# The product of probabilities and values with the probabilities stationary, in an encoder with linear and attention heads on one core

## The chip, the core and the metric

The kernel runs on one core of one Trainium2 chip. The metric is device time in microseconds of one execution, lower is better; the median of a few runs is taken. TensorE (PE) multiplies: it loads a stationary operand (PEld in the profile) and streams a moving one past it into PSUM. VectorE (DVE), ScalarE (ACT) and GpSimd (POOL) do the rest of the arithmetic, SyncE (SP) issues the DMAs.

## The reference

Two layers, each on 2048 tokens of 1024 channels. A normalised row is projected to several groups of columns; one half of the result is a gated mix inside chunks of 128 tokens, the other half is attention with 8 query heads of 64 channels on 2 key/value heads. Both halves are gated, projected back, normalised and added to the input. The part that is changed lies in the attention:

```python
def attend(qblk):
    sc = jnp.einsum('bqkgd,bskd->bkgqs', qblk, k).astype(jnp.float32) * scale
    p = jax.nn.softmax(sc, axis=-1).astype(v.dtype)
    return jnp.einsum('bkgqs,bskd->bqkgd', p, v)
...
y_b = gqa_axial_attention(q, k, v, q_norm_g[l], k_norm_g[l], tables) * jax.nn.silu(g_b)
y = jnp.concatenate([y_a, y_b], axis=-1)
out = jnp.einsum('bse,ed->bsd', y, w_out[l])
x = x + rmsnorm(out, post_g[l])
```

All of it is float32. The kernel reaches that precision by splitting operands in a high and a low half and adding the products of the halves.

## The kernel before

For each layer the kernel first projects (class `Project`) and keeps keys, values and queries; the values are scaled by a power of two and split in f16 halves (`scale_v`): `v16` holds, per key tile and key/value head, 64 high and 64 low columns. Then comes the attention (`attend`).

The attention runs over 32 units: 4 query blocks of 512 queries times 8 heads. A unit has 16 key tiles of 128 keys, so one layer has 512 steps (`k` in the loop). In each step TensorE makes scores with the keys on the partitions (`sp`, 128 keys by 512 queries, two matmuls), ACT takes the exponential twice, once to f16 (`p_hi`) and once to float32 (`p_f`), and POOL, in 15 of 100 steps DVE, forms the low half `p_lo` = `p_f` - `p_hi` (`sub_lo`). Three steps later (`LAG`, `LAG_LO`) the product with the values follows.

In that product the values are stationary and the probabilities stream, 512 columns at a time: per key tile one matmul with all 128 columns of `v16` and `p_hi`. It leaves in `s.po` a 128 by 512 result, the high values' part on one half of the partitions and the low values' part on the other. Every eight key tiles (`BATCH`) the products with `p_lo` follow, for the eight tiles at once, in products of 32 stationary columns: two of them per tile with the high values, into the right half of `s.po`, and two with a block of ones (`one_h`), into the bank `sums`, one for `p_lo` and one for `p_hi`. Four such products take four different strips of 32 columns of the array and run beside each other. So the denominators lie along the free axis of `sums`.

At the end of a unit `finish` evacuates: `half` (ACT) copies one half of `s.po`, `whole` (DVE) adds the other, `den_t` (DVE) transposes `sums` in blocks of 32, `den` (TensorE) sums and scales the denominators by small products with `two` into a bank `pd` with the queries on the partitions, `rden` (DVE) takes the reciprocal, `gate` (DVE) multiplies the gate by it, and for each pair of heads `gate_t` (TensorE) transposes the gate, `mul` (DVE) multiplies, and `split` (ACT and POOL) makes the halves `y_hi` and `y_lo`, which are stored.

Between these, spread over the steps, stand: the maxima of later units (`max_step`: one matmul `pmax` of 512 columns and one reduction on DVE, 16 per unit, in four of five steps), the output projection of the block before (`out_steps`, matmuls `pout`, taken from the list `fill`), and its normalisation (`post_steps`, one DVE instruction per step from `post_queue`).

The order of the work is written out by hand: `Pinned` keeps each instruction of TensorE, ACT, DVE and POOL in program order. In one step `k` it is: the scores and exponentials of `k`; POOL's `sub_lo`; one of `post_queue`; DVE's `sub_lo` of `k - 1`; what was put in `later` for this step, `max_step` first, then what `finish` put there; some of `fill`; then the product of step `k - 3`. `finish(u, k + 1)` is called at the last product of unit `u`.

PSUM has eight banks of 512 float32 columns: seven in the pool `ps` (scores, maxima, `po`, `pout` and others take one when they are allocated), and `sums`.

Of the kernel before, what the change touches and what calls it, by code (L numbers as in the profile page):

```python
# [26 lines left out]
NKV = 2  # L27
EPS = 1e-6
WB = 256
C_U, C_VA, C_GA, C_Q, C_K, C_GB = 0, 512, 1024, 1536, 2048, 2304  # L30
RSQRT_MAGIC = float(0x5F3759DF)
EXP_SHIFT = 4.1588830833596715
# [6 lines left out]
def encoder(ctx: ExitStack, tc, x, w_in, w_out, pre_g, post_g, ln_a_g, ln_a_b,  # L39
# [50 lines left out]
    make_identity(nc, ident)  # L90
    ones1 = const.tile([1, P], F32, name="ones1")
    nc.vector.memset(ones1, 1.0)
    two = const.tile([P, 32], F32, name="two")
    nc.vector.tensor_tensor(two, ident[:, 0:32], ident[:, 32:64], ALU.add)
    nc.vector.tensor_tensor(two, two, ident[:, 64:96], ALU.add)
    nc.vector.tensor_tensor(two, two, ident[:, 96:P], ALU.add)
    nc.vector.tensor_scalar_mul(two, two, 2.0)
    one_h = const.tile([P, 32], F16, name="one_h")
    nc.vector.memset(one_h, 1.0)

    ws_d = dram.tile([P, 2, NH * P], F32, name="ws_d")
    xn_d = [[dram.tile([P, D], F32, name=f"xn_{l}_{t}") for t in range(NT)] for l in range(DEPTH - 1)]
# [64 lines left out]
            while self.jobs:  # L167
                self.jobs.pop(0)[1]()

    sums = psum.tile([P, GRP], F32, name="sums")  # L170

    bg = Background()
    PASSES = ((0, 0), (0, 1), (1, 0))
# [1 line left out]
    class Project:  # L175
# [23 lines left out]

        def gains(self):  # L200
            l = self.l
            self.two = lay.tile([P, 32], F32, name="two_v")
            self.gain_q = lay.tile([P, 2, HD], F32, name="gain_q")
            self.gain_k = lay.tile([P, 2, HD], F32, name="gain_k")
            for gain, src in ((self.gain_k, k_norm_g), (self.gain_q, q_norm_g)):
                nc.sync.dma_start(gain[:, 0, :], src[l].partition_broadcast(P))
                gv = gain[:, 1, :].rearrange("p (a h i) -> p a h i", a=2, h=2)
                sv = src[l].rearrange("(a h i) -> a h i", a=2, h=2)
                for h in range(2):
                    nc.sync.dma_start(gv[:, :, h, :], sv[:, 1 - h, :].partition_broadcast(P))  # L210
            top = small.tile([P, 2], F32, name="g_top")
            e = small.tile([P, 1], F32, name="g_exp")
            inv = small.tile([P, 1], F32, name="g_inv")
            nc.vector.tensor_reduce(top[:, 0:1], self.gain_k[:, 0], AX.X, ALU.max)
            nc.vector.tensor_reduce(top[:, 1:2], self.gain_k[:, 0], AX.X, ALU.min, negate=True)
            nc.vector.tensor_tensor(e, top[:, 0:1], top[:, 1:2], ALU.max)
            ei = e.bitcast(I32)
            nc.vector.tensor_scalar(ei, ei, EXP_BITS, None, ALU.bitwise_and)
            nc.vector.tensor_scalar(ei, ei, float(97 << 23), float(157 << 23), ALU.max, ALU.min)
            nc.vector.tensor_scalar(inv.bitcast(I32), ei, -1.0, float(254 << 23), ALU.mult, ALU.add)  # L220
            nc.vector.tensor_scalar(self.gain_k, self.gain_k, inv, None, ALU.mult)
            nc.vector.tensor_scalar(self.gain_q, self.gain_q, e, HD ** -0.5, ALU.mult, ALU.mult)
# [266 lines left out]
        def scale_v(self):  # L489
# [18 lines left out]
            def scale():  # L508
                nc.vector.tensor_copy(e, self.top[:, 0:1])
                ei = e.bitcast(I32)  # L510
                nc.vector.tensor_scalar(ei, ei, EXP_BITS, None, ALU.bitwise_and)
                nc.vector.tensor_scalar(ei, ei, float(64 << 23), None, ALU.max)
                nc.vector.tensor_scalar(ei, ei, -1.0, V_TOP, ALU.mult, ALU.add)
                nc.vector.tensor_scalar(self.two, two, e, None, ALU.mult)

            def apply(i):
                def f():
                    t = slice(4 * i, 4 * i + 4)
                    hi = v16[:, t, :, 0:HD]
                    nc.scalar.activation(hi, v32[:, t], AF.Copy, scale=e)  # L520
                    nc.vector.scalar_tensor_tensor(v16[:, t, :, HD:2 * HD], v32[:, t], e, hi, ALU.mult, ALU.subtract)
                return f

            bg.add(6, spread)
            bg.add(11, spread_row)
            bg.add(13, scale)
            for i in range(NT // 4):
                bg.add(14 + i, apply(i))

        def run(self, kv, first, last_jobs, first_wo):  # L530

# [108 lines left out]
    T_DELAY = 9  # L640
    VA_DELAY = 9
    LAG = 3
    LAG_LO = 3
    BATCH = 8
    N_HI = 12
    N_F = 4
    N_LO = 12
    LAST_0 = 5
    LAST_1 = 12
    WS_DELAY = 18  # L650
# [1 line left out]
    def attend(l, kv, nxt):  # L652
# [74 lines left out]
        def finish(u, k):  # L727
# [1 line left out]
            qb, h = units[u]  # L729
            side = h % 2  # L730
            s, pr = state[u], pairs[u // 2]
            r, o = slice(side * HD, (side + 1) * HD), slice((1 - side) * HD, (2 - side) * HD)

            def half():
                if side == 0:
                    pr.o = f_t("o_pair")
                ACT.copy(pr.o[r], s.po[o])

            def whole():
                DVE.tensor_tensor(pr.o[r], s.po[r], pr.o[r], ALU.add)  # L740

            def den_t():
                s.ds = f_t("den")
                DVE.transpose(s.ds, sums)

            def den():
                s.pd = ps_t("pd")
                rows = s.ds.rearrange("p (t c j) -> p t c j", c=4, j=32)
                for c in range(4):
                    PE.matmul(s.pd[32 * c:32 * c + 32, 0:TPG], layers[l].two, rows[:, :, c, 0], start=True, stop=True)  # L750

            def rden():
                s.rd = small.tile([P, TPG], F32, name="rden")
                DVE.reciprocal(s.rd, s.pd[:, 0:TPG])

            def gate():
                gv = pr.gb[:, :, r]
                DVE.tensor_tensor(gv, gv, s.rd.unsqueeze(2).broadcast_to([P, TPG, HD]), ALU.mult)

            def gate_t():  # L760
                pr.pg = ps_t("pg")
                for j in range(TPG):
                    PE.transpose(pr.pg[:, j * P:(j + 1) * P], pr.gb[:, j, :], ident)

            def mul():
                DVE.tensor_tensor(pr.o, pr.pg, pr.o, ALU.mult)

            def split():
                y_hi = f_t("y_hi", dt=F32R)
                y_lo = f_t("y_lo", dt=F32R)  # L770
                ACT.copy(y_hi, pr.o)
                (DVE if u + 1 == len(units) else POOL).tensor_tensor(y_lo, pr.o, y_hi.bitcast(F32), ALU.subtract)
                if (qb, h) == units[-1]:
                    last_y.extend([y_hi, y_lo])
                    return
# [2 lines left out]
                nc.sync.dma_start(y_d[qb][:, c, 1], y_lo.bitcast(F32))  # L778

            if u + 1 == len(units):  # L780
                for n, f in ((0, den_t), (0, den), (1, rden), (1, gate), (1, half), (1, whole), (2, gate_t), (2, mul),
                             (2, split)):
                    at(k + n, f)
                return
            at(k, half)
            at(k, whole)
            at(k, den_t)
            narrow.append(den)
            at(k + BATCH, rden)
            at(k + BATCH + 1, gate)  # L790
            if side == 0:
                return
            at(k + BATCH + 3, gate_t)
            at(k + BATCH + 4, mul)
            at(k + BATCH + 5, split)

        narrow = []
        post_queue = []
        last_y = []

# [245 lines left out]
                f()  # L1046

        yield before, first_wo
        both = [w_t([P, 8, GRP], "p_parts", F16) for _ in range(3)]
        both = [b[:, n] for b in both for n in range(8)]  # L1050
        his, los = both[:N_HI], both[N_HI:]
        fs = w_t([P, N_F, GRP], "p_f", F32)
# [38 lines left out]
        def weight(k):  # L1091
            return 2 if k >= total - 2 * NT else 1

        end = total + LAG_LO

        def sub_lo(k, engine):
            engine.tensor_tensor(p_lo(k), p_f(k), p_hi(k), ALU.subtract)
# [18 lines left out]
        for k in range(end + 4):  # L1116
# [27 lines left out]
            if 0 <= kb < total:  # L1144
                u, i = kb // NT, kb % NT
                s = state[u]
                kv = units[u][1] // (NH // NKV)
                if i == 0:
                    s.po = ps_t("po")
                PE.matmul(s.po, v16[:, i, kv, :], p_hi(kb), start=(i == 0), stop=False)  # L1150
            kb = k - LAG_LO
            if 0 <= kb < total:
                u, i = kb // NT, kb % NT
                s = state[u]
                kv = units[u][1] // (NH // NKV)
                if i % BATCH == BATCH - 1:
                    while narrow:
                        narrow.pop(0)()
                    for n in range(i - BATCH + 1, i + 1):
                        kn = kb - i + n  # L1160
                        q = n % 2 * HD
                        for c in range(0, HD, 32):
                            PE.matmul(s.po[q + c:q + c + 32], v16[:, n, kv, c:c + 32], p_lo(kn),
                                      start=False, stop=(n >= NT - 2))
                        q = HD - q
                        PE.matmul(sums[q:q + 32], one_h, p_lo(kn), start=(n < 2), stop=(n >= NT - 2))
                        PE.matmul(sums[q + 32:q + HD], one_h, p_hi(kn), start=(n < 2), stop=(n >= NT - 2))
                if i == NT - 1:
                    finish(u, k + 1)
                    if units[u][1] == NH - 1 and u + 1 < len(units):  # L1170
# [33 lines left out]
    for l in range(DEPTH):  # L1204
# [1 line left out]
        kv = [k_t[:, 0], k_t[:, 1]]  # L1206
        v_t = big_t([P, 2, NT * NKV * HD], "v_st")
        kv.append(v_t.bitcast(F32)[:, 0].rearrange("p (t k d) -> p t k d", t=NT, k=NKV))
        kv.append(v_t.bitcast(F16)[:, 1].rearrange("p (t k d) -> p t k d", t=NT, k=NKV))
        att = attend(l, kv, layers[l + 1] if l + 1 < DEPTH else None)  # L1210
        layers[l].run(kv, layers[l].first, *next(att))
        for _ in att:
# [41 lines left out]
```

## Time and profile before

| | |
|---|---|
| median of 3 runs | 2740.2 us (2739.36 to 2740.77) |
| span of the profiled execution | 2737.6 us |
| TensorE busy | 2666.4 us (97%), 18234 matmuls |
| weight loads busy | 1773.2 us (65%) |
| DVE busy | 1858.2 us (68%) |
| ACT busy | 1523.9 us (56%) |
| POOL busy | 1296.1 us (47%) |

The span is the profiled execution's own time, from its first instruction to its last; the runs' median, which has also what lies around the span, is 2.6 us more. The first stretch of attention lies between about 627 and 1373 us of the span, the second between 1977 and 2716; the projections lie before each. The page's busy time of TensorE is a union of its matmuls' durations, which overlap (a matmul of 512 columns is shown with 0.38 us, while the next starts 0.22 after it); so its cost is read from the starts, or from the chain of work, which gives each step the time up to the next. In the profile L84 is the helper that records the pinned instructions, so groups are told apart by their tiles: `po<-p_parts,v_st` is the product with the values, `sums<-p_parts,one_h` that with the ones, `sp` the scores, `p_parts` the f16 halves `p_hi` and `p_lo`.

### The profile page before, as it was taken

What the parts mean: (1) busy time and instruction counts of PE and PEld (TensorE: products, weight loads), DVE (VectorE), ACT (ScalarE), POOL (GpSimd) and SP (SyncE); (2) the same over time, 40 slices, a digit from 0 to 9 for tenths busy, and PEclk for the clock granted to TensorE, in tenths of its full rate; (3) what the DMA queues carried; (4) which work ended last, traced back from release to release, by engine and by line L of the source; (5) the groups of instructions that cost most, each with busy time, mean ns of one, the idle gap of its engine ahead of it and who ended that gap; (6) DMA issues with size and microseconds to landing.
All of it is one profiled execution on the core that took longest, in us unless ns stands there. A gap on an engine that the chain in (4) does not pass through costs nothing.

```text
span 2737.6 us, 48445 instructions
## 1 busy us (share of the span) xinstructions
PE 2666.4 (97%) x18234; PEld 1773.2 (65%) x18234; DVE 1858.2 (68%) x3780; ACT 1523.9 (56%) x3023; POOL 1296.1 (47%) x1079
## 2 busy tenths in 40 slices
PE   7999999999999999999999999999999999999997
PEld 7998999764444444445599989997644444444444
DVE  7762888876666766666497538897766656666664
ACT  5221422118887777877642224221388878778774
POOL 1210121008786776777633011210377767767764
PEclk9999999999999999999999999999999999999998
DMA  4434422322232222222354434232312222221313
GB/s 137 149 98 122 161 80 84 107 75 84 81 91 66 76 84 84 90 81 84 125 169 138 122 115 144 74 121 71 109 51 81 79 71 70 83 75 48 114 46 132
DMA packets 275170, 264.78 MB, mean 97 GB/s; under 512 B 19188, under 2 KB 233332, under 8 KB 274936
## 3 DMA queue, kind: packets, MB, share of 16 engines
q1 hardware_dynamic: 274936, 261.70, 30.5%
q8 instruction: 143, 2.34, 0.4%
q14 instruction: 91, 0.75, 0.1%
HBM read 176.57 MB, written 85.07 MB: 96 GB/s over the span
## 4 chain that ended last, share of the span: by engine, by line
PE 81%; DVE 10%; ACT 5%; DMA 2%; issue 2%; POOL 1%; SPq 0%; DVEq 0%; POOLq 0%; ACTq 0%
PE pp L84 28%; PE sp L84 14%; PE pout L84 12%; PE po L84 12%; PE pmax L84 7%; PE sums L84 4%; PE pt L84 3%; ACT p_parts L84 2%; ACT p_f L84 2%; DVE fc L372 1%; DVE w_lo L277 1%; DVE mx L84 1%; DVE p_parts L84 1%; DVE o_t L84 1%; DVE mx L706 1%
## 5 line engine op out<-in xcount | busy, mean ns | idle before, releaser
L84 POOL TENSOR_TENSOR p_parts<-p_f,p_parts 128x512 f16<-128x512 f32 x872 | 1037.4, 1208 | 395.1 <-ACT p_f L84 295.5
L84 ACT ACTIVATE p_parts<-sp 128x512 f16<-128x512 f32 x1024 | 628.3, 614 | 295.7 <-PE sp L84 288.5
L84 DVE TENSOR_REDUCE mx<-pmax 128x1 f32<-128x512 f32 x768 | 511.2, 681 | 230.9 <-PE pmax L84 228.9
L84 PE MATMUL pout<-wo,y_t 128*128 128x512 f32 x1488 | 655.4, 504 | 1.0 <-ACT p_f L84 0.7
L84 PE MATMUL po<-p_parts,v_st 128*32 128x512 f16 (+1 forms) x3072 | 637.2, 382 | 0.2
L84 ACT ACTIVATE p_f<-sp 128x512 f32<-128x512 f32 x1024 | 629.9, 615 | 0.4 <-DVE p_parts L84 0.4
L84 PE MATMUL pp<-w_hi,hT 128*128 128x256 f32 x3584 | 496.7, 287 | 2.1 <-DVE k_t L405 1.1
L84 PEld LDWEIGHTS pp<-w_hi,hT 128*128 128x128 f32 x3584 | 457.3, 192 | 6.4 <-issue 1.3
L84 PE MATMUL pmax<-k_t,q_m 128*128 128x512 f16 x1024 | 388.9, 381 | 12.5 <-DVE mx L84 7.4
L84 PE MATMUL sp<-q_st,k_t 128*128 128x512 f16 x1024 | 389.2, 380 | 5.3 <-ACT p_f L84 2.9
L84 PEld LDWEIGHTS <-v_st 128*32 128x32 f16 (+1 forms) x3072 | 193.1, 96 | 308.4 <-issue 250.3
L84 PE MATMUL sp<-q,k_t 66*128 66x512 f16 x1024 | 390.1, 381 | 0.0
L84 PEld LDWEIGHTS pout<-wo,y_t 128*128 128x128 f32 x1488 | 280.7, 190 | 134.2 <-issue 14.9
L84 PEld LDWEIGHTS <-k_t 128*128 128x128 f16 (+1 forms) x2048 | 191.3, 98 | 184.1 <-issue 71.1
L477 POOL TENSOR_TENSOR fl<-fa,fh 128x512 fp32r<-128x512 f32 x32 | 42.7, 1335 | 539.6 <-ACT fh L476 496.0
L84 PE MATMUL pp<-hT,w_hi 128*128 128x512 f32 x1024 | 273.1, 413 | 0.0
L84 PE MATMUL pp<-w_lo,hT 128*128 128x256 f32 x1792 | 260.0, 288 | 0.0
L84 PE MATMUL sums<-p_parts,one_h 128*32 128x512 f16 x2048 | 241.8, 379 | 0.0
L84 PEld LDWEIGHTS pp<-w_lo,hT 128*128 128x128 f32 x1792 | 232.9, 192 | 1.0
L84 PEld LDWEIGHTS pp<-hT,w_hi 128*128 128x128 f32 x1024 | 192.8, 189 | 35.1
L706 DVE TENSOR_REDUCE mx<-pmax 128x1 f32<-128x512 f32 x256 | 172.5, 687 | 49.1 <-PE pmax L84 47.5
L84 PEld LDWEIGHTS <-q_m 128*128 128x128 f16 x1024 | 99.8, 98 | 142.6 <-issue 41.8
(165 smaller groups left out, 2778.1 us busy)
## 6 DMA issues: line engine op xcount, KB each, us to landing
w_raw<-in_w_in_dram SPq DMA_DIRECT2D x28, 1024.0 KB
y_t<-y_d SPq DMA_DIRECT2D x56, 512.0 KB
w_raw<-in_w_in_dram SPq DMA_DIRECT2D x32, 512.0 KB
x_t<-in_x_dram SPq DMA_DIRECT2D x16, 512.0 KB
z_d<-fb SPq DMA_DIRECT2D x32, 256.0 KB
gb_d<-fa SPq DMA_DIRECT2D x32, 256.0 KB
fb<-z_d SPq DMA_DIRECT2D x32, 256.0 KB
y_d<-fh SPq DMA_DIRECT2D x32, 256.0 KB
```

What stands on the lines that cost most here:

```text
L84: return tc.keep_in_program_order(call(*args, **kw))
L277: nc.vector.tensor_tensor(lo[:, sl], raw[:, sl], hi.bitcast(F32)[:, sl], ALU.subtract)
L372: nc.vector.tensor_tensor(t2[:, :, :, lo:lo + 16], qn[:, :, :, hi:hi + 16], tbi[:, :, 1:2, lo:lo + 16].broadcast_to([P, 2, n, 16]), ALU.mult)
L477: nc.gpsimd.tensor_tensor(lo, th, hi.bitcast(F32), ALU.subtract)
L706: dve.tensor_reduce(s.mx[:, j, c:c + 1], ps, AX.X, ALU.max)
```

## The change

The operands of the product change places. The probabilities become stationary: for each key tile and each of the four tiles of 128 queries (`j`), the 128 by 128 block of `p_hi` is loaded and 129 columns of `v16` stream past it, and the block of `p_lo` is loaded and 65 columns stream past it. `v16` now holds, per key tile and head, 64 low columns, 64 high columns, a column of ones and a spare one (`VW` = 130, `VN` = 129); the product with `p_lo` uses the high values and the ones. So the queries lie on the partitions of the result, with the denominator as a column of its own, and nothing is batched over eight tiles.

A unit's result has 4 x 129 = 516 columns. Three of the four query tiles take a bank from the pool `ps` (`AV_BANKED`), the fourth takes one of three slots of 129 columns in the bank `po_3`, which replaces `sums`; units take the slots in turn. `finish` now copies the low values' part with ACT, scales the denominators with DVE (`evac`), one step later adds the high values' part (`add`), one later takes the reciprocal and multiplies the gate (`gate`), one later multiplies (`mul`), and for each pair transposes the result instead of the gate (`trans`) and splits it; the low half is made by DVE, from PSUM, and no longer by POOL. `den_t`, `den`, `one_h` and the block `two` go. The pools of halves shrink from 12 to 8 each (`N_HI`, `N_LO`), which frees one of the seven weight buffers. The values are split from the last four key tiles to the first.

```diff
-    sums = psum.tile([P, GRP], F32, name="sums")
+    po_3 = psum.tile([P, GRP], F32, name="po_3")
...
-                nc.vector.tensor_scalar(self.two, two, e, None, ALU.mult)
+                nc.vector.tensor_scalar(self.two, e, 2.0, None, ALU.mult)
...
-                    hi = v16[:, t, :, 0:HD]
+                    hi = v16[:, t, :, HD:2 * HD]
                     nc.scalar.activation(hi, v32[:, t], AF.Copy, scale=e)
-                    nc.vector.scalar_tensor_tensor(v16[:, t, :, HD:2 * HD], v32[:, t], e, hi, ALU.mult, ALU.subtract)
+                    nc.vector.scalar_tensor_tensor(v16[:, t, :, 0:HD], v32[:, t], e, hi, ALU.mult, ALU.subtract)
+                    nc.vector.memset(v16[:, t, :, 2 * HD:VW], 1.0)
...
-                bg.add(14 + i, apply(i))
+                bg.add(14 + i, apply(NT // 4 - 1 - i))
...
-    LAG_LO = 3
-    BATCH = 8
-    N_HI = 12
+    AV_BANKED = 3
+    N_HI = 8
     N_F = 4
-    N_LO = 12
+    N_LO = 8
...
+            def evac():
                 if side == 0:
-                    pr.o = f_t("o_pair")
...
+                    pr.o = f_t("o_pair").rearrange("p (t e) -> p t e", t=TPG)
                 s.rd = small.tile([P, TPG], F32, name="rden")
-                DVE.reciprocal(s.rd, s.pd[:, 0:TPG])
+                for b, js in s.banks:
+                    ACT.copy(pr.o[:, js, r], b[:, :, 0:HD])
+                    DVE.tensor_scalar(s.rd[:, js], b[:, :, 2 * HD], layers[l].two, None, ALU.mult)
+
+            def add():
+                for b, js in s.banks:
+                    DVE.tensor_tensor(pr.o[:, js, r], b[:, :, HD:2 * HD], pr.o[:, js, r], ALU.add)
 
             def gate():
+                DVE.reciprocal(s.rd, s.rd)
                 gv = pr.gb[:, :, r]
                 DVE.tensor_tensor(gv, gv, s.rd.unsqueeze(2).broadcast_to([P, TPG, HD]), ALU.mult)
...
+            def mul():
+                DVE.tensor_tensor(pr.o[:, :, r], pr.o[:, :, r], pr.gb[:, :, r], ALU.mult)
+
+            def trans():
+                pr.py = ps_t("py")
                 for j in range(TPG):
-                    PE.transpose(pr.pg[:, j * P:(j + 1) * P], pr.gb[:, j, :], ident)
...
+                    PE.transpose(pr.py[:, j * P:(j + 1) * P], pr.o[:, j], ident)
 
             def split():
...
-                ACT.copy(y_hi, pr.o)
-                (DVE if u + 1 == len(units) else POOL).tensor_tensor(y_lo, pr.o, y_hi.bitcast(F32), ALU.subtract)
+                ACT.copy(y_hi, pr.py)
+                DVE.tensor_tensor(y_lo, pr.py, y_hi.bitcast(F32), ALU.subtract)
...
+            at(k, evac)
+            at(k + 1, add)
+            at(k + 2, gate)
+            at(k + 3, mul)
             if side == 0:
                 return
...
+            at(k + 5, trans)
+            at(k + 6, split)
...
-        both = [w_t([P, 8, GRP], "p_parts", F16) for _ in range(3)]
+        both = [w_t([P, 8, GRP], "p_parts", F16) for _ in range(2)]
...
                 if i == 0:
-                    s.po = ps_t("po")
-                PE.matmul(s.po, v16[:, i, kv, :], p_hi(kb), start=(i == 0), stop=False)
...
+                    po = ps_t("po")[:, 0:AV_BANKED * VN].rearrange("p (t e) -> p t e", e=VN)
+                    p3 = po_3[:, u % 3 * VN:(u % 3 + 1) * VN].rearrange("p (t e) -> p t e", e=VN)
+                    s.banks = [(po, slice(0, AV_BANKED)), (p3, slice(AV_BANKED, TPG))]
+                    s.av = [po[:, j] for j in range(AV_BANKED)] + [p3[:, 0]]
+                for j in range(TPG):
+                    js = slice(j * P, (j + 1) * P)
+                    first = i == 0 and j in (0, AV_BANKED)
+                    PE.matmul(s.av[j], p_hi(kb)[:, js], v16[:, i, kv, 0:VN], start=first, stop=False,
+                              skip_group_check=True)
+                    PE.matmul(s.av[j][:, HD:VN], p_lo(kb)[:, js], v16[:, i, kv, HD:VN], start=False,
+                              stop=i == NT - 1, skip_group_check=True)
                 if i == NT - 1:
                     finish(u, k + 1)
```

More of the change, by code (lines that the diff above doesn't have):

```diff
@@ L29 @@
 WB = 256
+VW = 2 * HD + 2
+VN = 2 * HD + 1
 C_U, C_VA, C_GA, C_Q, C_K, C_GB = 0, 512, 1024, 1536, 2048, 2304
@@ L92, in encoder @@
     nc.vector.memset(ones1, 1.0)
[L93 to L99, printed above, removed]
     ws_d = dram.tile([P, 2, NH * P], F32, name="ws_d")
@@ L201, in gains @@
             l = self.l
-            self.two = lay.tile([P, 32], F32, name="two_v")
+            self.two = lay.tile([P, 1], F32, name="two_v")
             self.gain_q = lay.tile([P, 2, HD], F32, name="gain_q")
@@ L731, in finish @@
             s, pr = state[u], pairs[u // 2]
-            r, o = slice(side * HD, (side + 1) * HD), slice((1 - side) * HD, (2 - side) * HD)
-            def half():
+            r = slice(side * HD, (side + 1) * HD)
+            def evac():
                 if side == 0:
-                    pr.o = f_t("o_pair")
[L737 to L752, printed above, removed]
-                s.rd = small.tile([P, TPG], F32, name="rden")
-                DVE.reciprocal(s.rd, s.pd[:, 0:TPG])
+                    pr.o = f_t("o_pair").rearrange("p (t e) -> p t e", t=TPG)
+                s.rd = small.tile([P, TPG], F32, name="rden")
+                for b, js in s.banks:
[4 more added lines that the diff above has]
+                    DVE.tensor_tensor(pr.o[:, js, r], b[:, :, HD:2 * HD], pr.o[:, js, r], ALU.add)
             def gate():
+                DVE.reciprocal(s.rd, s.rd)
                 gv = pr.gb[:, :, r]
                 DVE.tensor_tensor(gv, gv, s.rd.unsqueeze(2).broadcast_to([P, TPG, HD]), ALU.mult)
-            def gate_t():
-                pr.pg = ps_t("pg")
+            def mul():
+                DVE.tensor_tensor(pr.o[:, :, r], pr.o[:, :, r], pr.gb[:, :, r], ALU.mult)
+            def trans():
+                pr.py = ps_t("py")
                 for j in range(TPG):
-                    PE.transpose(pr.pg[:, j * P:(j + 1) * P], pr.gb[:, j, :], ident)
-            def mul():
-                DVE.tensor_tensor(pr.o, pr.pg, pr.o, ALU.mult)
+                    PE.transpose(pr.py[:, j * P:(j + 1) * P], pr.o[:, j], ident)
             def split():
@@ L780, in finish @@
             if u + 1 == len(units):
-                for n, f in ((0, den_t), (0, den), (1, rden), (1, gate), (1, half), (1, whole), (2, gate_t), (2, mul),
-                             (2, split)):
+                for n, f in ((0, evac), (0, add), (1, gate), (1, mul), (2, trans), (2, split)):
                     at(k + n, f)
                 return
[L785 to L790, printed above, removed]
+            at(k, evac)
+            at(k + 1, add)
+            at(k + 2, gate)
+            at(k + 3, mul)
             if side == 0:
                 return
[L793 to L797, printed above, removed]
+            at(k + 5, trans)
+            at(k + 6, split)
         post_queue = []
@@ L1092, in weight @@
             return 2 if k >= total - 2 * NT else 1
-        end = total + LAG_LO
+        end = total + LAG
         def sub_lo(k, engine):
@@ L1148, in attend @@
                 if i == 0:
-                    s.po = ps_t("po")
-                PE.matmul(s.po, v16[:, i, kv, :], p_hi(kb), start=(i == 0), stop=False)
[L1151 to L1167, printed above, removed]
+                    po = ps_t("po")[:, 0:AV_BANKED * VN].rearrange("p (t e) -> p t e", e=VN)
[9 more added lines that the diff above has]
+                              stop=i == NT - 1, skip_group_check=True)
                 if i == NT - 1:
@@ L1208, in encoder @@
         kv.append(v_t.bitcast(F32)[:, 0].rearrange("p (t k d) -> p t k d", t=NT, k=NKV))
-        kv.append(v_t.bitcast(F16)[:, 1].rearrange("p (t k d) -> p t k d", t=NT, k=NKV))
+        v_h = v_t.bitcast(F16).rearrange("p a n -> p (a n)")[:, 4 * NT * NKV * HD - NT * NKV * VW:]
+        kv.append(v_h.rearrange("p (t k d) -> p t k d", t=NT, k=NKV))
         att = attend(l, kv, layers[l + 1] if l + 1 < DEPTH else None)
```

## The prediction

> **What bounds the kernel now.** I read the page's busy shares first, then its chain of work, then the chain in a short stretch of the attention, then the timeline there.
>
> ```profile
> span 2737.6 us, 48445 instructions
> PE 2666.4 (97%) x18234; PEld 1773.2 (65%) x18234; DVE 1858.2 (68%) x3780; ACT 1523.9 (56%) x3023; POOL 1296.1 (47%) x1079
> PEclk9999999999999999999999999999999999999998
> PE 81%; DVE 10%; ACT 5%; DMA 2%; issue 2%; POOL 1%; SPq 0%; DVEq 0%; POOLq 0%; ACTq 0%
> PE pp L84 28%; PE sp L84 14%; PE pout L84 12%; PE po L84 12%; PE pmax L84 7%; PE sums L84 4%; PE pt L84 3%; ACT p_parts L84 2%; ACT p_f L84 2%; DVE fc L372 1%; DVE w_lo L277 1%; DVE mx L84 1%; DVE p_parts L84 1%; DVE o_t L84 1%; DVE mx L706 1%
> ```
>
> TensorE is busy nearly everywhere at full granted clock and carries the chain, so a microsecond of its work saved or of its idling added in the attention is a microsecond of time. All sums are against this span; the median of the runs, 2740.2, is 2.6 us above it and takes the same differences. The attention is two stretches of some 740 us. The view of busy time by stretch, here for the first and third query block of the first layer, and the sum over the eight blocks of both layers:
>
> ```profile
> 627.00:796.00 169.00, 164.90 (x1166) 72.57 (x1159) 110.08 (x176) 144.04 (x289) 132.01 (x112) 1.00 0.23 72
> 985.00:1177.00 192.00, 189.02 (x1284) 90.24 (x1283) 130.56 (x264) 151.11 (x310) 138.88 (x115) 1.00 0.27 85
> sum 1485.00, PE 1462.35 PEld 702.95 DVE 932.74 ACT 1159.13 POOL 1060.02; mean PE 182.79 PEld 87.87 DVE 116.59 ACT 144.89 POOL 132.50
> ```
>
> The columns are length, then PE, PEld, DVE, ACT and POOL. With 128 tiles in a block a tile takes 1.32 to 1.5 us of TensorE, while ACT uses 1.1 to 1.2 of it, POOL 1.03 to 1.09 and DVE 0.9 to 1.0. So ACT is the next limit, about 0.2 us per tile away.
>
> **What the old product costs.** The chain over one group of eight tiles (start, length, what), which TensorE fills without a gap:
>
> ```profile
> 1202.02 0.23 PE po L84
> 1202.25 0.18 PE pd L84 x8
> 1202.42 0.22 PE po L84 x2
> ...
> 1204.17 0.54 PE sp L84 x2
> ...
> 1205.62 0.43 PE sp L84 x2
> ```
>
> Each tile pays 0.23 for its high product. Each eighth tile pays the batch of low products and sums: from 1202.25 to 1204.17 plus the 0.11 by which the next score pair (0.54 against 0.43) is late, 2.03 us with the denominator's eight small products. That is 1024 x 0.23 + 128 x 2.03 = 495 us, 0.48 per tile, all on the path and all removed.
>
> **What the new product costs.** Eight matmuls per tile, four of 129 and four of 65 columns, each with its own 128x128 weight load of f16. The price of a column comes from streams without a gap, in the chain:
>
> ```profile
> 131.81 14.40 PE pp L84 x120
> 2710.38 0.44 PE pg L84 x4
> 1357.11 1.39 PE pout L84 x6
> ```
>
> 256 columns of pp take 0.120, 512 of pout 0.23: 0.42 ns per column and 13 ns on top for f32. A pair of f16 scores, 1024 columns, takes 0.43: 0.42 ns per column and almost nothing on top. So 129 + 65 columns are 81.5 ns if the weight loads hide. Whether they do is seen in the loads' rows and in their starts:
>
> ```profile
> 1192.77 0.10 PEld L84 LDWEIGHTS <-v_st 128*128 128x128 f16 x1 [0.26 <-issue]
> 1192.77 0.39 PE L84 MATMUL po<-p_parts,v_st 128*128 128x512 f16 x1
> 1192.78 0.31 PEld L84 LDWEIGHTS <-k_t 128*128 128x128 f16 x2
> 1193.00 0.38 PE L84 MATMUL sp<-q_st,k_t 128*128 128x512 f16 x1
> 1193.21 0.38 PE L84 MATMUL sp<-q,k_t 66*128 66x512 f16 x1
> ```
>
> An f16 load lasts 0.10, but the next begins 0.01 after it, and the product behind two such loads is late by 0.02 at most (0.23 to the next start, against 0.21 where only one load lies between). So a load occupies the array for some 15 ns and can run beside the product ahead of it; a 65-column product lasts 27 ns, which covers it. Bounds of the pair: 81.5 ns with all hidden, 112 ns with both loads open. I take 87 (3 ns on top of each product), nearest the f16 score rows; the four transposes pg, each with a load of twice the bytes, also show no load in their 0.11. A tile is then 4 x 87 + 13 ns for the open load behind pout, 0.36 us, 1024 x 0.36 = 370 us: **125 us gained**, 23 at the upper bound of 112 ns.
>
> A rule speaks against this. The Trainium skill, "TensorE: Matmul & The Clock Gate", section "Back-to-back issue gap", gives about 81 ns per product for a stream of load and product pairs of 128 columns; an estimate from that page is 81 + 54 = 135 ns per pair and some 70 us lost on the product. The score rows above, with a load each and nothing on top, do not agree at 512 columns; no run here shows 128.
>
> **What the new evacuation makes wait.** Three of the four query tiles of a unit (129 columns each) accumulate in a bank of their own; the fourth goes to one of three slots of po_3, and the three slots lie in one bank. At the end of unit u the program's order is: last product of u; in the next iteration the evacuation of po, then of po_3 (ACT copy, DVE column of denominators); then the first product of u+1, which writes another slot of the same bank; one iteration later the DVE add on po_3; then the second product of u+1. If accesses of different engines to one bank are kept in program order, TensorE waits for the copy and the column in the first iteration, and for the add in the second, each time with the scores of the next tile queued behind it. In before the accumulator's next use came in another buffer and sums was next written eight tiles later, so no row shows such a wait. What stands ahead of the evacuation is seen at this unit end:
>
> ```profile
> 1191.87 0.39 PE L84 MATMUL sp<-q_st,k_t 128*128 128x512 f16 x1
> 1192.10 0.38 PE L84 MATMUL sp<-q,k_t 66*128 66x512 f16 x1
> 1192.32 0.38 PE L84 MATMUL pmax<-k_t,q_m 128*128 128x512 f16 x1
> 1192.52 0.60 ACT L84 ACTIVATE p_parts<-sp 128x512 f16<-128x512 f32 x1 [0.60 <-PE sp L84]
> 1192.73 0.69 DVE L84 TENSOR_REDUCE mx<-pmax 128x1 f32<-128x512 f32 x1 [0.29 <-PE pmax L84]
> 1193.01 0.59 ACT L84 ACTIVATE p_f<-sp 128x512 f32<-128x512 f32 x1
> 1193.62 0.58 ACT L84 COPY o_pair<-po 64x512 f32<-64x512 f32 x1
> 1193.73 1.16 POOL L84 TENSOR_TENSOR p_parts<-p_f,p_parts 128x512 f16<-128x512 f32 x1 [0.15 <-PE sp L84]
> ```
>
> ```profile
> L84 PE MATMUL pout<-wo,y_t 128*128 128x512 f32 x1488 | 655.4, 504 | 1.0 <-ACT p_f L84 0.7
> L84 ACT COPY o_pair<-po 64x512 f32<-64x512 f32 x64 | 37.1, 580 | 12.0 <-PE po L84 10.5
> L391 ACT COPY v_st<-pp 128x256 f32<-128x256 f32 x16 | 6.0, 372 | 21.9 <-PE pp L84 21.9
> L84 DVE RECIPROCAL rden<-pd 128x4 f32<-128x4 f32 x64 | 11.1, 174 | 1.4 <-PE pd L84 1.3
> L367 DVE TENSOR_TENSOR fc<-pp,rs_y 128x512 f32<-128x512 f32 x32 | 21.9, 685 | 0.6
> L367 DVE TENSOR_TENSOR fc<-pp,rs_y 128x256 f32<-128x256 f32 x16 | 6.7, 418 | 0.4
> L84 DVE STREAM_TRANSPOSE den<-sums 128x512 f32<-128x512 f32 x64 | 45.3, 708 | 3.6 <-PE po L84 2.7
> L84 DVE TENSOR_TENSOR o_pair<-po,o_pair 64x512 f32<-64x512 f32 x64 | 44.1, 689 | 97.5 <-ACT o_pair L84 96.5 <-DMA q<-q_d 0.8
> L84 DVE TENSOR_TENSOR gb<-gb,rden 128x256 f32<-128x256 f32 x64 | 43.7, 683 | 0.5
> ```
>
> The first wait: from the start of the scores the copy begins 1.75 later (1191.87 to 1193.62), behind both exponentials. By the two copy rows (0.81 ns per element) 192 elements take 0.32 and 64 take 0.22: 2.29. The column, like the reciprocal, 0.17 and hand-overs: 2.53. TensorE's own work to that point is 0.43 scores, 0.18 pmax (0.22 in four of five tiles), 0.32 pout (1488 of them in 1024 tiles, some in the last steps, so 1.4 a tile of 0.23), and 0.26 for the three tiles ahead: 1.19. It idles **1.34 us**. The second: the maximum's reduction stands ahead of the adds and ends 1.55 after the scores' start (1191.87 to 1193.42); by the two L367 rows (1.04 ns per element) the adds take 0.35 and 0.22: 2.15 with the hand-over, against 1.23 of TensorE's work, 0.92; where no pmax is due, nothing. On average **0.70 us**. Together 2.04 at each of 62 unit ends (31 per layer): **126 us lost**. The bounds are 0, if columns of one bank may be used independently, and 2.6 if ACT or DVE is a step late.
>
> The Trainium skill, "PSUM — Partial Sum Buffer", section "PSUM bank collisions raise a hardware error", asks that PSUM be guarded by bank and quadrant and not by address, which is the ordering assumed here; no run here shows it yet.
>
> **Everything else.** DVE per unit, by the rows above: out go a transpose of 0.71, an add of 0.69 and half of a 512-wide multiply (0.34); in come two columns of 0.17, adds of 0.57, a 256-wide multiply like that of gb (0.68) and half of the 512-wide low split that leaves POOL (0.34): 1.93 for 1.74. The 0.2 us per unit of 16 tiles are hidden by DVE's 0.3 us and more of slack per tile; without that cover they cost 64 x 0.2 = 13 us. POOL loses 30 splits. ACT's two copies (0.54) replace one of 0.58. The low product now waits for its low half each tile: POOL ends 3.02 us after the scores' start (1193.73 + 1.16 from 1191.87), and the product comes three tiles of 1.3 and 0.75 later, 1.6 us to spare; in the first two dozen tiles of a layer, where TensorE has no fill, POOL may pace it, 0 to 5 us per layer, against which ACT's present delays in the first block (169 - 165 = 4 us per layer) are absorbed by the new idling. I put both at 0. SP's queue issues the same loads; one freed weight buffer can only bring them earlier. The values' memsets and the last unit's tail change less than 2 us.
>
> **Sum:** 2740.2 - 125 + 126 + 0 = **2741 us**: no change, out of two large terms that nearly cancel.
>
> **Rivals.**
> - No wait at the bank: TensorE's 125 us come through, 2615. Against it: the first product of a unit stands between the evacuation and the add in the program. For it: no row of before shows such a wait. 12%.
> - Only the first wait (the add slips ahead of the next product): 62 x 1.34 = 83, so 2740 - 125 + 83 = 2698. For it: pmax is not due in one tile of five, and DVE is idle a third of the time. 15%.
> - Slower, by one mechanism: the two weight loads of a pair stay open, because a 27 ns product leaves no time to start the next load. At 112 ns the gain is 23, and the waits shrink by 62 x 0.13 = 8: 2740 - 23 + 118 = 2835. Against it: the loads' starts above. It decides from about 87 ns a pair on, the forecast's own value, where the gain falls below the waits; each further ns costs 4 us. Anywhere between 92 and 115 ns: 20%.
> - More of each load shows than its 15 ns. The rows' upper end is the 0.11 by which the scores are late behind a batch of narrow products, where the load could not run ahead. With 27 ns a load, nearer the lower end as there is no change of form here, a pair is 81.5 + 54 = 135 ns, a tile 0.55, 567 us in all, 72 lost; the waits shrink by 62 x 0.26 = 16: 2740 + 72 + 110 = 2922. The score and transpose rows speak against it. It would be the page's rule above. 7%.
> - The forecast, 2715 to 2770 with its own errors of 5 ns a pair and 0.3 us a wait: 46%.
>
> **Numbers.** A measurement of this kernel tells about 0.2%, 5.5 us, from no change. The forecast's own range splits into 0.15 faster, 0.11 same and 0.20 slower. With the rivals (0.12 + 0.14 faster, 0.01 same, 0.20 + 0.07 slower) that is 0.41, 0.12 and 0.47. The range takes all but this last kind of load and the far end of the open loads: 2612 to 2825.
>
> **What the changed profile would show.** The product: 129- and 65-column rows with starts 57 and 30 ns apart, a tile's eight in 0.35. The waits: TensorE or its weight loads idle at po_3, once released by the column of denominators (about 1.3 us) and once by the add (0.9), some 62 and 50 times; if these are absent, the first rival holds. ACT's share in the attention should stay near 78% if the forecast is right and rise to some 85% if the waits are absent. What would make me wrong: pairs above 95 ns, waits that are not there, or a wait I do not name, most of all for the low half when POOL runs behind.

## The result, and the profile after

The changed kernel takes 2757.7 us (median; 2756.4 to 2759.6) against 2739.8 before in the same runs: a ratio of 1.0064, with a 95% interval of 1.0049 to 1.0078. So it is slower by some 18 us. In the later runs of the experiments the kernel before took 2742.3 and 2741.9 us, so a difference between a time of one group of runs and a time of another carries some 2 us. The forecast was 2741 with a range of 2612 to 2825: the time lies in the range, 17 us above the point, and on the side that held 0.47 of the chance.

The page of the changed kernel: span, busy shares, granted clock in 40 slices, chain by engine.

```profile
span 2755.3 us, 53763 instructions
PE 2585.4 (94%) x20794; PEld 1943.9 (71%) x20794; DVE 1840.4 (67%) x3973; ACT 1527.0 (55%) x3087; POOL 1250.9 (45%) x1049
PEclk9999999999999999999999999999999999999999
PE 72%; DVE 13%; ACT 8%; issue 3%; DMA 2%; POOL 1%; SPq 0%; DVEq 0%; POOLq 0%; ACTq 0%
```

TensorE is busy for 81 us less (2585.4 against 2666.4) and the span is 18 us longer: it now waits. Where, the view of waits of TensorE says (engine, tile, releaser: us in total, times, longest). First the largest row of before that lies in the attention, then the rows of the product after:

```profile
PE pmax L84 <- DVE mx L84: 7.4, 11, 2.3
```

```profile
PE po L86 <- DVE rden L86: 71.5, 62, 2.0
PE po L86 <- DVE o_pair L86: 38.2, 47, 3.2
PE po L86 <- DVE p_parts L86: 5.4, 6, 3.3
PE po L86 <- POOL p_parts L86: 4.0, 5, 1.7
```

The first two rows after are the two waits of the forecast: 62 for the column of denominators, 47 for the add, 109.7 us together. The view names a tile after its role, so po_3 stands under `po`. From the first scores of an attention to its last product, both layers together, TensorE is idle for 22.2 us before and for 123.1 after. One unit end in the timeline of the changed kernel (start, duration, engine), other instructions left out:

```profile
1067.15 0.38 PE L86 MATMUL sp<-q_st,k_t 128*128 128x512 f16 x1
1067.79 0.60 ACT L86 ACTIVATE p_parts<-sp 128x512 f16<-128x512 f32 x1 [0.39 <-PE sp L86]
1068.28 0.44 PE L86 MATMUL po<-v_st,p_parts 128*128 128x129 f16 x6
1068.28 0.59 ACT L86 ACTIVATE p_f<-sp 128x512 f32<-128x512 f32 x1
1068.76 0.45 ACT L86 COPY o_pair<-po 128x192 f32<-128x192 f32 x2
1069.12 0.34 DVE L86 TENSOR_SCALAR rden<-po,two_v 128x3 f32<-128x3 f32 x2 [0.17 <-ACT o_pair L86]
1069.52 0.25 PE L86 MATMUL po<-v_st,p_parts 128*128 128x129 f16 x2 [0.80 <-DVE rden L86]
1069.60 0.38 PE L86 MATMUL sp<-q_st,k_t 128*128 128x512 f16 x1
1070.45 0.69 DVE L86 TENSOR_REDUCE mx<-pmax 128x1 f32<-128x512 f32 x1 [0.87 <-PE pmax L86]
1070.72 0.44 PE L86 MATMUL po<-v_st,p_parts 128*128 128x129 f16 x6
1071.06 0.48 DVE L86 TENSOR_TENSOR o_pair<-po,o_pair 128x192 f32<-128x192 f32 x2
1071.59 0.25 PE L86 MATMUL po<-v_st,p_parts 128*128 128x129 f16 x2 [0.44 <-DVE o_pair L86]
```

A row of six products, then a pause, then the two of the fourth query tile: that is the mark of the wait. The copies begin 1.61 after the scores' start, behind both exponentials, the columns end 0.70 later, and TensorE goes on at once. One step later the reduction of the maximum stands ahead of the adds, and the pause repeats.

The product itself, on the chain of the changed kernel a few tiles earlier:

```profile
1065.01 0.46 PE pout L86 x2
1065.47 0.36 PE po L86 x8
1065.84 0.44 PE sp L86 x2
```

Eight products with their eight loads in 0.36 us, as forecast; from start to start the trace has a median of 59 ns for 129 columns and 29 for 65.

What was not forecast is in the column of the granted clock, the third from the end, in the view by stretch. Before, the two attentions and one short stretch:

```profile
627.00:1373.00 746.00, 731.97 (x5024) 351.54 (x5017) 480.23 (x887) 585.11 (x1180) 533.01 (x445) 1.00 0.27 86
1977.00:2716.00 739.00, 730.38 (x5024) 351.41 (x5024) 452.51 (x804) 574.03 (x1143) 527.00 (x445) 1.00 0.24 78
667.00:674.00 7.00, 6.86 (x62) 2.93 (x61) 4.62 (x10) 5.50 (x12) 4.79 (x5) 1.00 0.45 152
```

After, the two attentions, two short stretches, and a longer one ahead of these:

```profile
627.00:1373.00 746.00, 683.62 (x6213) 427.82 (x6212) 465.46 (x967) 586.52 (x1212) 509.51 (x431) 0.97 0.26 81
1977.00:2716.00 739.00, 680.30 (x6246) 426.00 (x6245) 447.21 (x897) 581.78 (x1186) 510.91 (x435) 0.99 0.25 79
667.00:674.00 7.00, 6.21 (x32) 3.39 (x32) 3.95 (x8) 2.40 (x5) 2.45 (x2) 0.52 0.00 0
735.00:742.00 7.00, 4.56 (x21) 2.34 (x21) 3.34 (x8) 2.69 (x7) 2.30 (x2) 0.51 0.02 4
640.00:665.00 25.00, 21.60 (x209) 13.00 (x208) 14.18 (x28) 20.80 (x45) 18.05 (x16) 1.00 0.07 24
```

The clock is full, and then half for 3.4 or 6.8 us. At half clock the matmuls come at about half the rate too: 32 in the 7 us from 667 on, where 209 in 25 us make 58 in 7. The trace's record of the clock has 13 such stretches in the attentions, 58 us in all; before had none between its first 40 us and its tail. The slices of the page, in tenths, hide them.

### The profile page after: what moved, and what is told of

It reads as the page before. It is cut to its first block, busy times and chain, and to the rows that moved or that the text cites. A ratio compares the mean times of both kernels' runs of the same rounds, so it can differ in the third digit from the quotient of the medians.

```text
span 2755.3 us, 53763 instructions
## 1 busy us (share of the span) xinstructions
PE 2585.4 (94%) x20794; PEld 1943.9 (71%) x20794; DVE 1840.4 (67%) x3973; ACT 1527.0 (55%) x3087; POOL 1250.9 (45%) x1049
## 4 chain that ended last, share of the span: by engine, by line
PE 72%; DVE 13%; ACT 8%; issue 3%; DMA 2%; POOL 1%; SPq 0%; DVEq 0%; POOLq 0%; ACTq 0%
PE pp L86 26%; PE sp L86 14%; PE po L86 11%; PE pout L86 11%; PE pmax L86 7%; ACT p_f L86 3%; ACT p_parts L86 3%; PE pt L86 3%; DVE fc L367 2%; DVE mx L86 2%; DVE w_lo L272 1%; DVE o_pair L86 1%; DVE o_t L86 1%; DMA fa<-in_rope_dram 1%; DVE rden L86 1%
## 5 line engine op out<-in xcount | busy, mean ns | idle before, releaser
L86 ACT ACTIVATE p_parts<-sp 128x512 f16<-128x512 f32 x1024 | 621.2, 607 | 313.3 <-PE sp L86 310.8
L86 PEld LDWEIGHTS <-p_parts 128*128 128x128 f16 x8192 | 406.2, 98 | 408.0 <-issue 358.2
L86 DVE TENSOR_REDUCE mx<-pmax 128x1 f32<-128x512 f32 x768 | 519.7, 685 | 254.5 <-PE pmax L86 252.0
L86 PE MATMUL po<-v_st,p_parts 128*128 128x129 f16 (+1 forms) x8192 | 561.0, 209 | 120.2 <-DVE rden L86 71.5
L86 PE MATMUL pout<-wo,y_t 128*128 128x512 f32 x1488 | 665.8, 511 | 1.5 <-DVE mx L86 1.5
L86 ACT ACTIVATE p_f<-sp 128x512 f32<-128x512 f32 x1024 | 619.4, 605 | 0.0
L86 PE MATMUL sp<-q,k_t 66*128 66x512 f16 x1024 | 396.2, 387 | 0.0
L701 DVE TENSOR_REDUCE mx<-pmax 128x1 f32<-128x512 f32 x256 | 172.6, 687 | 49.0 <-PE pmax L86 47.5
L271 ACT CAST w_hi<-w_raw 128x1024 fp32r<-128x1024 f32 (+1 forms) x92 | 89.6, 1013 | 124.7 <-PE pp L86 93.1
L86 DVE TENSOR_TENSOR p_parts<-p_f,p_parts 128x512 f16<-128x512 f32 x152 | 113.1, 744 | 41.8 <-ACT p_f L86 41.5
```

Of the source, the lines that this page charges most:

```text
L86: return tc.keep_in_program_order(call(*args, **kw))
L271: nc.scalar.copy(hi[:, sl], raw[:, sl])
L701: dve.tensor_reduce(s.mx[:, j, c:c + 1], ps, AX.X, ALU.max)
```

## Experiments

The theory: the product saves what it should, and is lost again at po_3, where two waits per unit end are set by the order of the work around one bank, and by the halved clock that these waits bring. Rivals: ACT and DVE, the next bound, would take the gain anyway; the halved clock comes from the short products and not from the waits.

**A bank of its own for the fourth query tile** (e1_pool).

```diff
-    po_3 = psum.tile([P, GRP], F32, name="po_3")
-        return psum.tile([P, GRP], F32, name=name, tag="ps", bufs=7)
+        return psum.tile([P, GRP], F32, name=name, tag="ps", bufs=8)
-                    p3 = po_3[:, u % 3 * VN:(u % 3 + 1) * VN].rearrange("p (t e) -> p t e", e=VN)
+                    p3 = ps_t("po3")[:, 0:VN].rearrange("p (t e) -> p t e", e=VN)
```

Expected: 

> The fourth query tile's 129 columns get a bank of their own from the pool (8 buffers in place of 7 and po_3), so no unit writes a bank that another engine still reads. Theory: the changed kernel pays 110 us of waits at po_3 (71.5 + 38.2 in its view of waits) and some 25 us of halved TensorE clock that these waits bring; both go: 2758 - 135 = 2623, to 2645 if the pool gets tight; granted clock back at 0.997. Rival 1: the waits only show what ACT and DVE would cost anyway, as they are the next bound: not under 2700. Rival 2: the halved clock comes from the short products, not from the waits: clock stays at 0.986 and the time is 2645 to 2650.

Measured: 2630.8 us, 0.9593 of before (0.9577 to 0.9609), mean clock 0.994. Of TensorE's waits at the product only those for the low halves are left:

```profile
PE po L86 <- DVE p_parts L86: 4.6, 4, 3.3
PE po L86 <- POOL p_parts L86: 4.0, 5, 1.8
```

Both rivals fall: 127 us go with the shared bank alone, with the same products in the same order, and the clock comes back with them (0.994 against 0.986).

**The shared bank kept, but emptied at once** (e2_early). Copy, column and add of po_3 are issued right behind the unit's last product; those of the larger bank stay where they were.

```diff
+            def small_bank():
+                alloc()
+                copy_of(1)
+                add_of(1)
...
+            small_bank()
             if u + 1 == len(units):
```

Expected: 

> po_3 stays, but its copy, column and add are issued right behind a unit's last product, ahead of the next exponentials, the next pmax and the evacuation of po. Theory: copy, column and add (0.22 + 0.17 + 0.22 and hand-overs) end some 0.95 us after the next scores begin, TensorE comes to po_3 after 1.19: no wait is left, 2620 to 2640, clock 0.997. Rival 1 (ACT and DVE are the bound anyway): not under 2700. A rival in which the bank itself, not the order of the work, makes the wait: waits at po_3 stay above 0.5 us per unit and the time above 2690.

Measured: 2632.3 us, 0.9600 of before (0.9586 to 0.9614), clock 0.995. The waits:

```profile
PE po L86 <- DVE p_parts L86: 5.0, 6, 3.3
PE po L86 <- DVE o_pair L86: 4.7, 11, 1.0
PE po L86 <- POOL p_parts L86: 4.0, 5, 1.7
PE po L86 <- DVE rs_o L86: 3.9, 6, 0.9
```

and a unit end in its timeline:

```profile
999.84 0.21 ACT L86 COPY o_pair<-po 128x64 f32<-128x64 f32 x1
1000.09 0.22 DVE L86 TENSOR_SCALAR rden<-po,two_v 128x1 f32<-128x1 f32 x1 [0.38 <-ACT o_pair L86]
1000.23 0.21 DVE L86 TENSOR_TENSOR o_pair<-po,o_pair 128x64 f32<-128x64 f32 x1
1001.25 0.33 ACT L86 COPY o_pair<-po 128x192 f32<-128x192 f32 x1
```

All that the bank needs is over in 0.60 us, and the copy stands ahead of both exponentials of the step, where in the changed kernel it stood behind them. So one bank with three slots costs next to nothing (1.5 us more than e1_pool); the place in the program did. The three slots are one tile of the program as well as one bank, and no run has three tiles in one bank: whether the program orders by bank or by tile stays open.

**One wait in place of two** (e4_onewait): the evacuation stays one step after the unit's end, but takes po_3 first and adds it there (`small_bank` and `copy_of` are those of e2_early).

```diff
             def evac():
+                small_bank()
+                copy_of(0)
```

Expected: 

> The evacuation stays in the step after the unit's end but takes po_3 first, and adds it there too, so that TensorE can wait for it only once. Theory: copy, column and add end 2.45 us after the scores' start, against 1.19 of TensorE's work: one wait of 1.2 to 1.3 us per unit end in place of 1.15 + 0.62; 30 us of waits gone and 10 to 25 of halved clock, 2705 to 2725. If both waits are set by the load of ACT and DVE and not by the order: no change, 2750 to 2760.

Measured: 2694.2 us, 0.9826 of before (0.9811 to 0.9840), clock 0.995; below what was expected. The wait is one per unit end, 1.06 us and not 1.2 to 1.3, and the clock is as good as with no wait:

```profile
PE po L86 <- DVE o_pair L86: 66.0, 62, 1.9
```

Of the 63 us gained 44 are waiting (109.7 to 66.0); the clock record has 7 us of half clock in the attentions in place of 58. The remainder, some 20 us, fits the clock: 51 us less at half clock are worth at most 26. The next runs measure it apart.

**Work in the waits** (e3_filler, e5_fill1, e6_fill2). TensorE runs products that nobody reads where it would idle: ahead of the first product of a unit in po_3, ahead of the second, or both.

```diff
                     first = i == 0 and j in (0, AV_BANKED)
+                    if j == AV_BANKED and u > 0 and (i == 0 or (i == 1 and k in max_at)):
+                        idle = ps_t("idle")
+                        for _ in range(5 if i == 0 else 3):
+                            PE.matmul(idle, k_st[:, kv, 0:P], s.qs, start=True, stop=True)
```

(e5_fill1 has only the case `i == 0`, e6_fill2 only the other; `max_at` holds the steps in which a `pmax` is due.)

Expected of both: 

> The waits stay; while TensorE would idle it runs products whose result nobody reads: five of 512 columns (1.08 us) ahead of the first product of a unit in po_3, three (0.65 us) ahead of the second where a pmax is due. Theory that the halved clock follows from the idling: clock back at 0.995 or more and the time falls by 15 to 27 us in spite of the added work, to 2731 to 2743. Rival 2 (clock falls for another reason, or its loss is no time): no gain, 2755 to 2770, clock 0.986.

Of the first alone: 

> The changed kernel with idle products only ahead of a unit's first product in po_3 (five of 512 columns); the second wait, for the add, stays idle. Theory: the clock falls where two waits, together some 2 us, come within one or two tiles, not for one alone, as the kernel with a single wait of 1.06 us shows (two half-clock windows in the attention against thirteen): with one wait covered the clock is back at 0.994 and the time as with both covered, 2743 to 2748. Rival: each wait alone takes its part of the clock: clock about 0.990, 2749 to 2755.

Of the second alone: 

> The counterpart: idle products (three) only ahead of the second product in po_3; the first wait of 1.15 us stays idle. Theory (two waits close together): clock back at 0.994, 2743 to 2750. Rival (each wait its part, the longer one more): clock 0.988 to 0.990, 2751 to 2757.

Measured: both 2744.6 us (1.0010 of before, 1.0001 to 1.0019), the first 2746.2 (1.0017, 1.0008 to 1.0026), the second 2746.1 (1.0017, 1.0007 to 1.0027); clocks (median of the ten runs of each) 0.995, 0.993, 0.992. None of these intervals touches that of the changed kernel (1.0049 to 1.0078): more work on the engine that is the bound makes the kernel 12 to 13 us faster. The groups of the idle products in e3_filler and e6_fill2 have 454 and 144 of them; each is shown with 379 ns, though they start 216 ns apart:

```profile
L86 PE MATMUL idle<-q_st,k_t x454: 376/379/382, 639.5 to 2688.1; 128*128 128x512 f16 x152
```

```profile
L86 PE MATMUL idle<-q_st,k_t x144: 377/379/634, 643.4 to 2647.0; 128*128 128x512 f16 x144
```

After the count stand the shortest, the median and the longest in ns. TensorE's waits at po_3 in e3_filler, then in e6_fill2, where the longer one is still idle:

```profile
PE po L86 <- DVE o_pair L86: 12.7, 10, 2.8
PE po L86 <- DVE rden L86: 9.4, 24, 0.9
```

```profile
PE po L86 <- DVE rden L86: 71.6, 62, 2.0
PE po L86 <- DVE o_pair L86: 12.3, 9, 2.8
```

The clock record has 20, 34 and 27 us at half in the attentions (the profile of e5_fill1 is of its slowest run, 2750.8 us). So covering either wait is worth nearly as much as covering both. The times of the theory hold (2743 to 2748 and 2743 to 2750); the clocks, 0.993 and 0.992 in the median, lie between its 0.994 and the rivals' 0.990 and less.

Its mechanism, two waits close together, is only one case of what the traces show. The stretches of half clock begin, within one trace, at whole multiples of 3.413 us from one another. In the ten traces 43 of them begin in the attentions; in the 3.41 us ahead of each, TensorE is idle for 1.57 to 2.98 us. Of the more than 4100 other such windows at full clock none has more than 1.78 us, and only seven have more than 1.57. So what counts is how much idling, as the trace shows it, falls into one window, with the limit at about half of the window; into how many waits it is split does not matter. Of the 13 stretches of the changed kernel six follow a window with both waits (at 782.9, for one, 1.05 and 0.66 us), five a window with one long wait at po_3 (at 823.9 that for the column, 1.88 us), and two a wait for a low half. The fillers take away those with both: all 7 stretches of e5_fill1 and all 8 of e6_fill2 follow a single wait.

**The price of the short product** (e7_short, on e2_early; a single run). It leaves half of the low halves' part out of the sum.

```diff
-                    PE.matmul(s.av[j][:, HD:VN], p_lo(kb)[:, js], v16[:, i, kv, HD:VN], start=False,
+                    PE.matmul(s.av[j][:, VN - 33:VN], p_lo(kb)[:, js], v16[:, i, kv, VN - 33:VN], start=False,
```

Expected: 

> On the kernel that empties po_3 at once (2632 us): the products with the low halves of the probabilities stream 33 columns in place of 65, so half of that part of the sum is left out. If the columns set the price of the short product (29 ns from start to start), it falls by 32 x 0.42 = 13 ns, 4096 of them by 55 us, to about 2580, unless ACT, at 1.1 us a tile, takes over at about 2590. If the load of the next block sets it, it stays near 27 to 29 ns and the time within 10 us of 2632.

Measured: 2616.8 us, 15.5 less than e2_early. On the chain, e2_early and then e7_short:

```profile
1000.92 0.37 PE po L86 x8
1002.40 0.36 PE po L86 x8
```

```profile
1000.80 0.34 PE po L86 x8
1002.26 0.34 PE po L86 x8
```

Half the columns save 20 to 30 ns of 360, not 52. From start to start the short product takes a median of 26 ns with 33 columns and 29 with 65; the long one beside it falls from 59 to 56, which is as much again. So neither case is quite right: by the columns alone, 0.42 ns each, 33 would take 14 ns, so something else holds the product at 26, and 65 columns lie just above that. Whether it is the load or the product itself, this run does not tell. It is near what the Trainium skill states in "TensorE: Matmul & The Clock Gate", section "Wait — 56ns, not 53.3ns?": no less than about 25 ns from start to start.

**Four steps behind the scores** (e8_lag4, on e2_early): `LAG = 4` in place of 3.

Expected: 

> On the kernel that empties po_3 at once: the product follows the scores by four steps in place of three. Theory: what is left of TensorE's waits for the low halves (5.0 us behind DVE and 4.0 behind POOL, at the beginning of a layer) shrinks: 2622 to 2630. If these waits only move to another place, 2630 to 2636.

Measured: 2625.7 us, 0.9575 of before (0.9561 to 0.9589), clock 0.996; the fastest of the kernels that form the whole sum. TensorE's waits at the product:

```profile
PE po L86 <- DVE o_pair L86: 6.8, 9, 1.4
PE po L86 <- POOL p_parts L86: 3.9, 4, 1.3
PE po L86 <- DVE rs_o L86: 3.0, 4, 0.9
```

The wait for DVE's low halves (5.0) is gone, that for POOL's stays (3.9 against 4.0): the first part of the theory holds, the second does not. The time is that of the theory, but only in part for its reason: in the attentions TensorE idles 2.6 us less than in e2_early (25.8 against 28.4), as other waits grow, and is busy 7.5 us less, with no half clock there in place of 10 us.

## Why the prediction was right, and by how much its terms were off

The mechanism and the signs of both large terms were as forecast; no step of it failed. Three sizes were off by 13 to 30 us and nearly cancel, so that the time came within 17 us of the point is in part luck. The sizes below are from the attentions, first scores to last product, both layers: 1488.1 us before (1465.9 busy, 22.2 idle), 1506.3 after (1383.2 and 123.1), 1382.0 in e2_early (1353.6 and 28.4).

- *The product.* Its cost per tile, 0.36 us, is on the chain to the hundredth, and the rivals with open loads (112 or 135 ns a pair) are refuted by starts 59 and 29 ns apart. But in e2_early, which has next to no wait for po_3, TensorE does 112 us less work than before and not 125. Where the other 13 went is not traced; the 10 us that e2_early spends at half clock explain 5 at most. The waits for the low halves, which I put at nothing, are 9.4 us after (5.4 and 4.0) and 9.0 in e2_early.
- *The waits.* 71.5 + 38.2 = 110 us, not 126, and in all TensorE idles 101 us more than before, as small waits of before are gone. The first is 1.15 a unit end, not 1.34: the two copies overlap and take 0.45, not 0.54, and begin 1.61 after the scores at the unit end shown, not 1.75. The second came 47 times (50 forecast), 0.81 each (0.92). That the next unit's product waits until the other engines have read po_3, which I could only assume, is in the rows: with separate banks they are gone, with the order changed nearly. "Only the first wait" and "no wait" were wrong as rivals, and became e4_onewait and e2_early. ACT's share of the attention is 78% as forecast (1178 of 1506 us), and 85% in e2_early.
- *The clock.* I priced the idling and not what it does to the work after it. For the same products TensorE is busy 30 us longer after than in e2_early (1383.2 against 1353.6). The record has 58 us at half clock against 10, and 48 us at half cost at most 24. The rest, some 6 us, is not settled; a part may be that the trace shows a matmul longer than the step to the next start, so that a pause begins later in it than the work ends. The fillers agree in size: 38 us less at half clock (58 to 20), worth at most 19, gained 13.

Together: 112.3 us of work gained, 100.9 of idling and 29.6 of clock and pauses lost, 18.2 us slower, where the forecast had 125 gained and 126 lost.

The rule of the Trainium skill that spoke against the change ("TensorE: Matmul & The Clock Gate", section "Back-to-back issue gap"), with 81 ns for a load and product of 128 columns, does not describe this stream: 129 columns with their own load took a median of 59 ns, and 56 with the shorter product of e7_short. The Trainium skill's rule in "PSUM — Partial Sum Buffer", section "PSUM bank collisions raise a hardware error", to guard by bank and not by address, agrees with the waits at po_3, where the product writes other columns than those that are read; that a guard by tile would do the same here, no run rules out.

## What to carry to other kernels

Treat slots in one PSUM bank as one resource: here, where the next unit wrote another slot, the reads of the last one had to end first. So they belong directly behind its last write and ahead of unrelated work in the queues of the engines that read. Price an order by what stands ahead of the releasing instruction in its queue (here two exponentials and a reduction), not by its own 0.2 us. And price idling on TensorE a second time through its clock where pauses within some 3.4 us add up to half of that (here from 1.57 us on, in every case above 1.78).

## What the runs showed of the hardware that I had not expected

- After idling of 1.57 to 2.98 us within one window of 3.41 us the granted clock fell to half for 3.4 or 6.8 us, 43 times in ten traces, whether it came in one pause or in two; 11 of the 13 in the changed kernel go back to po_3. With one wait of 1.06 us on average per unit end (e4_onewait) there were two, one behind a longer wait for po_3 (1.90 us) and one behind a wait for a low half. The Trainium skill, "TensorE: Matmul & The Clock Gate", section "HAM oscillation — how this bites in real kernels", sets the limit at idle gaps over about 3.4 us. The stretches of 3.4 us agree with its window, but no wait at the product was longer than 3.3 us, so that rule would have forecast no loss.
- An f16 product with its own 128-column load starts 26 ns (33 columns), 29 ns (65) or 59 ns (129) after the last, as medians; nine in ten of the 129-column ones take 68 ns or less. By 0.42 ns a column 65 and 129 would take 27 and 54, so at these sizes all but 2 to 5 ns of the loads hide.
- Filling a wait with products that nobody reads paid: 12 us for 144 of them in e6_fill2, 13 for 454 in e3_filler.
